# Two kinds of transpose leave TensorE: values and keys turned in 32x32 squares by VectorE and placed by GpSimd, with another window of dense steps before the corner products

## The chip, the cores and the metric

The kernel runs on one core of one Trainium2 chip. The number that counts is the device time of one execution in microseconds (us), as the median of several runs. A change of this size is read against the spread of these runs.

## The reference, cut to what matters

One layer of a two-branch backbone runs over 384 tokens (128 of context, 256 latent). One wide input projection feeds a bidirectional RWKV-7 scan (branch A) and a gated short convolution (branch B). Each branch is projected to the model width, the two are merged by gates and projected once more.

```python
z = h @ w_in                                   # 384 x 2048 by 2048 x about 22900, the bulk of the work
def step(S, inp):                              # branch A, per head, per direction, per token
    r_t, w_t, k_t, v_t, a_t, b_t = inp
    sa = einsum('dbhij,dbhj->dbhi', S, a_t)
    S = S * w_t[..., None, :] + sa[..., :, None] * b_t[..., None, :] + v_t[..., :, None] * k_t[..., None, :]
    y = einsum('dbhij,dbhj->dbhi', S, r_t)
y_a = (groupnorm(y) * lnx_g + lnx_b + bonus) * silu(g_a) @ w_out_a
y_b = (b_gate * conv3(c_gate * x_b) * silu(g_b)) @ w_out_b
out = x + gate * ((sigmoid(m_a) * y_a + sigmoid(m_b) * y_b) @ w_o)
```

The scan has 32 heads of 64 channels and two directions; its final context states are outputs too.

## The kernel before, in words

**Dense steps.** All large products run in one stream of dense steps. One step is three 128x128 by 128x384 matmuls (L81, L82, L83: high part by high part, high by low, low by high; the split into parts is made by ScalarE at L88 and VectorE at L89 for weights, elsewhere for data). A pair of weight column blocks is 32 steps. The stream holds pairs called rk (r and k of a block), gv (gate and v), bc, bx, bg, gb (branch B), ma, mb (merge gates), and at the end ob (output projection of B). What consumes a finished pair (L467 to L485 and others, VectorE and ScalarE) is issued beside it.

**Blocks.** The scan runs in 16 blocks of two heads. The sequence is cut into 6 chunks of 64 tokens, in each of 2 directions. Within a chunk the recurrence is a triangular system. For one block the work in program order is:

- `prep_b`: products pA of keys and queries (L703, TensorE), masked into the tile A by VectorE (L709, four for each direction). The two 32x32 diagonal triangles of each chunk go through DRAM into a tile U with the triangles on 48 partitions (`ui`, L713; `U`, L719). VectorE inverts them in 30 rounds of a product (L724) and a sum (L726): this is called the solve below. The result goes back through DRAM into A (`uo`), and VectorE turns one half of it into the tile x11 (L737, two instructions). Meanwhile GpSimd scales the keys `bk` in place (L716).
- `prep_c`: TensorE transposes the values v and the reversed values vr (L763, 2 x 3 of 128x128) and the scaled keys bk (L772, 10 of 128x128) by multiplying with the identity; ScalarE copies the results from PSUM into the lower half of `sav` (L765) and into `bt` (L773). Each group is followed by one dense step.
- `prep_a` of the next block: its keys, decays and queries.
- `scan`: products pav of A with the values (L850), the corner of the inverse (pH, L842, reads x11; later pX), a bonus product, and then two interleaved chains over the chunks (po L804, pq L821, pu L828) that carry the state; between these stand a few dense steps each.
- `norm` and, in the next block, `finish`: group norm, transposition back (py, L936), the gate (L939, L940), and a store to DRAM.

**Order.** TensorE's instructions keep the order in which the program issues them. `ds_.go(n)` issues n dense steps at that place. The constant `WINDOW` sets how many stand between the second pA and the corner of a block (`FIRST` and `LAST` add to it in the first and the last block). On the other engines a scheduler orders instructions by their readiness in its own model and by priority; an engine then runs them in that fixed order.

**The gate's wait.** Before `prep_a(b + 1)` the program issues dense steps until the pair gv of block b is done. In all, between the second pA and pav there are 87 dense steps in blocks 2 to 14 (six behind pA, `PB1`, and 81 more), 101 in block 1, 110 in block 0 and 102 in block 15.

**The tail.** After block 15's `finish` the rows of branch A come back from DRAM, one load (L507, tile `yst_a`, three buffers), one cast and one split (L509, tile `yal`) for each of 16 rows, and feed the output projection oa (tile d_oa). What is left of the pairs ob runs ahead of it.

Of the kernel before, what the change touches and what calls it, by code (L numbers as in the profile page):

```python
# [15 lines left out]
P = 128  # L16
D = 2048
KC = 16
T = 384
# [37 lines left out]
def hybrid_step(ctx, tc, cst, x_prompt, x_sample, state_f, state_b, c, c_ctx, ada_w, ada_b, norm_g,  # L57
# [35 lines left out]
    PB0, PB1, H0, H1, CH0, CH1 = 14, 6, 3, 4, 2, 4  # L93
    PRO, WINDOW, FIRST, LAST = 32, 80, 24, 16

# [313 lines left out]
    def tmp(nm):  # L409
        return box["sp"].tile([P, T], F32, tag="t", name=nm, bufs=8)  # L410
# [231 lines left out]
    def prep_k(b, o):  # L642
# [6 lines left out]
        for d in range(2):  # L649
# [15 lines left out]
            o["bn"].append(aa)  # L665

    def prep_b(b, o):

# [28 lines left out]
        for d in range(2):  # L697
# [7 lines left out]
            for n0, w in ((0, 4), (4, 2)):  # L705
                mk = cs[:, m0:m0 + P].rearrange("p (w t) -> p w t", t=C).unsqueeze(1).broadcast_to([P, w, 2, C])
                for h in range(2):
                    f0 = NCH * d + n0
                    V.tensor_tensor(A[:, :, f0:f0 + w, hss[h]].rearrange("p w n t -> p n w t"),  # L709
                                    pas[h, n0][:, 0:w, :].rearrange("p n (w t) -> p n w t", t=C), mk, ALU.mult)  # L710
            yield PB1
# [3 lines left out]
        for d in range(2):  # L715
            G.tensor_tensor(o["bk"][d][:], o["bk"][d][:], o["ep"][d][:, :, C:C + 1].broadcast_to([P, NCH, P]), ALU.mult)  # L716

# [21 lines left out]
    def prep_c(b, o):  # L739

        r, v, A = r_[b], v_[b], o["A"]

        s_in = sp.tile([P, 2, C], F32, tag="s_in", name=f"s_in_{b}")
        for d in range(2):
            for h in range(2):
                for jb in range(2):
# [3 lines left out]
                                      [:, :, 32 * jb:32 * jb + 32])  # L750

        sav = sp.tile([P, 2 * NCH, P], F32, tag="sav", name=f"sav_{b}")
        bt = sp.tile([P, 2 * NCH, P], F32, tag="bt", name=f"bt_{b}")
        o["sav"], o["bkt"] = sav, bt
        for d in range(2):
            if d == 0:
                src = v
            else:
                src = tmp(f"vr_{b}")
                S.copy(src[:], v[:, ::-1])  # L760
            pv = bank(f"pv_{b}_{d}")
            for q in range(3):
                TE.transpose(pv[:, q, :], src[:, q * P:(q + 1) * P], ident)  # L763
            for e in range(2):
                S.copy(sav[C:P, NCH * d + e:NCH * d + NCH:2, :], pv[C * e:C * e + C, 0:3, :])  # L765
            yield 1
        for d in range(2):

            for n0, n1 in (((0, 4), (4, 5)), ((0, 3), (4, 6)))[d]:
                pb = bank(f"pb_{b}_{d}_{n0}")  # L770
                for n in range(n0, n1):
                    TE.transpose(pb[:, n - n0, :], o["bk"][d][:, n, :], ident)  # L772
                S.copy(bt[:, NCH * d + n0:NCH * d + n1, :], pb[:, 0:n1 - n0, :])  # L773
                yield 1
        ks = o["kd"]
# [166 lines left out]

    def drive(gen, prio=0, at=None, fn=None):
        n = i = 0
        while True:
            if i == at:
                fn()
            i += 1
            with tc.high_priority(offset=prio):
                u = next(gen, None)  # L950
            if u is None:
                return n
            ds_.go(u)
            n += u
# [3 lines left out]
    drive(prep_a(0, cur))  # L958
    prep_k(0, cur)
    prev = None  # L960
    for b in range(NB):
# [10 lines left out]
        n = drive(prep_c(b, cur))  # L972
        nxt = {}
        if b < NB - 1:
            while f"gv{b}" not in ds_.done:
                ds_.go(1)
                n += 1
            n += drive(prep_a(b + 1, nxt))
        w = WINDOW + (FIRST if b == 0 else LAST if b == NB - 1 else 0)
        if n < w:  # L980
# [6 lines left out]

        drive(scan(b, cur), 300, 3 if b < NB - 1 else None, keys)
        norm(b, cur)
# [182 lines left out]
```

## Time and profile before

| what | value |
| --- | --- |
| median of 3 runs | 2237.07 us (2235.28 to 2239.02) |
| the profiled execution's own time | 2234.36 us |
| its span in the profile | 2232.6 us |
| TensorE busy | 2173.1 us, 97% |
| VectorE busy | 1553.3 us, 70% |
| ScalarE busy | 1013.5 us, 45% |
| GpSimd busy | 115.7 us, 5% |
| granted TensorE clock | 0.998 |

PE is TensorE, DVE VectorE, ACT ScalarE, POOL GpSimd, SP the engine that issues most transfers. A row of the timeline gives the start in us from the span's start, the busy time, the engine, the line of the kernel, the operation, the tiles (written <- read), the shapes, the count of instructions in a row, and in brackets how long the engine stood idle before it and what ended that. A row of the groups gives, after the count, the busy time and the mean of one instruction in ns, and then the idle time of the engine just before these instructions with its main releaser. Matmuls overlap: a dense matmul is shown with 0.33 us, while the next one starts 0.174 us later.

### The profile page before, as it was taken

Reading aid. Unit: us, or ns where it says so; the run is one execution under the profiler, and the core shown is the slowest. Engines: PE = TensorE matmul, PEld = TensorE weight load, DVE = VectorE, ACT = ScalarE, POOL = GpSimd, SP = SyncE. Lnnn points to the kernel's source line nnn. Section 1 sums busy time; section 2 is a strip of 40 time slices with the busy share of each in tenths; the row PEclk is TensorE's granted clock in tenths of the full one; section 3 lists DMA queues with packets and bytes.
Section 4 is the critical chain, followed back from the end, with each engine's and each line's share of the span. In section 5 each row is a group of like instructions: output and inputs, shape, how many; then the busy total and the mean of one; then the engine's idle time right before and its main releaser. Section 6 shows DMA issues by size and latency. Waiting matters only on the chain.

```text
span 2232.6 us, 40518 instructions
## 1 busy us (share of the span) xinstructions
PE 2173.1 (97%) x16020; PEld 2062.7 (92%) x16020; DVE 1553.3 (70%) x3240; ACT 1013.5 (45%) x1784; POOL 115.7 (5%) x113
## 2 busy tenths in 40 slices
PE   5999999999999999999999999999999999999998
PEld 3589999999999999999999999999999999998988
DVE  3259567787878878777878787887777785444354
ACT  4245435454545454444445454546454633333333
POOL 2000000000000000000000000000000000000000
PEclk9999999999999999999999999999999999999999
DMA  9974454444343435343444434344445464886633
GB/s 338 346 211 128 131 141 116 116 117 118 108 132 107 130 100 131 106 130 100 121 108 127 112 107 133 107 122 126 124 118 139 144 196 143 294 281 233 220 132 113
DMA packets 426574, 335.25 MB, mean 150 GB/s; under 512 B 82496, under 2 KB 408720, under 8 KB 425488
## 3 DMA queue, kind: packets, MB, share of 16 engines
q1 hardware_dynamic: 424896, 330.91, 50.2%
q8 instruction: 126, 2.06, 0.4%
q10 hardware_dynamic: 432, 1.57, 0.2%
q14 instruction: 64, 0.52, 0.1%
q0 software_dynamic: 1056, 0.19, 0.1%
HBM read 305.80 MB, written 26.21 MB: 149 GB/s over the span
## 4 chain that ended last, share of the span: by engine, by line
PE 74%; DVE 12%; DMA 6%; ACT 4%; issue 2%; SPq 1%; POOL 0%; POOLq 0%; DVEq 0%; ACTq 0%
DMA raw_adah<-in_ada_w_dram 4%; PE d_rk L81 3%; PE d_rk L82 3%; PE d_rk L83 3%; PE d_gv L81 3%; PE d_gv L82 3%; PE d_gv L83 3%; PE d_oa L81 2%; PE pA L703 2%; PE d_oa L83 2%; PE d_oa L82 2%; PE d_mb L81 2%; PE d_mb L83 2%; PE d_mb L82 2%; PE d_bc L81 2%
## 5 line engine op out<-in xcount | busy, mean ns | idle before, releaser
L724 DVE TENSOR_TENSOR ut<-U 48x30 f32<-48x30 f32 (+14 forms) x480 | 154.8, 323 | 18.3 <-DMA U<-ui 5.5
L81 PE MATMUL d_rk<-h_hi,whi_rk 128*128 128x384 f32 x480 | 161.7, 337 | 0.6 <-ACT lst L554 0.6
L726 DVE TENSOR_TENSOR U<-U,ut 48x30 f32<-48x30 f32 (+14 forms) x480 | 154.5, 322 | 11.1
L81 PE MATMUL d_gv<-h_hi,whi_gv 128*128 128x384 f32 x480 | 160.6, 335 | 0.0
L82 PE MATMUL d_rk<-h_lo,whi_rk 128*128 128x384 f32 x480 | 160.5, 334 | 0.0
L83 PE MATMUL d_rk<-h_hi,wlo_rk 128*128 128x384 f32 x480 | 160.4, 334 | 0.0
L83 PE MATMUL d_gv<-h_hi,wlo_gv 128*128 128x384 f32 x480 | 160.4, 334 | 0.0
L82 PE MATMUL d_gv<-h_lo,whi_gv 128*128 128x384 f32 x480 | 160.4, 334 | 0.0
L88 ACT CAST whi_gv<-raw_gv 128x1024 fp32r<-128x1024 f32 (+1 forms) x64 | 64.0, 999 | 139.6 <-PE d_rk L82 100.0
L88 ACT CAST whi_rk<-raw_rk 128x1024 fp32r<-128x1024 f32 x60 | 63.0, 1054 | 110.8 <-PE d_rk L82 34.7
L89 DVE TENSOR_TENSOR wlo_rk<-raw_rk,whi_rk 128x1024 fp32r<-128x1024 f32 x60 | 72.9, 1218 | 45.3 <-ACT whi_rk L88 35.6
L81 PE MATMUL d_bc<-h_hi,whi_bc 128*128 128x384 f32 x256 | 92.2, 360 | 0.0
L81 PE MATMUL d_gb<-h_hi,whi_gb 128*128 128x384 f32 x256 | 92.2, 360 | 0.0
L81 PE MATMUL d_bg<-h_hi,whi_bg 128*128 128x384 f32 x256 | 92.2, 360 | 0.0
L81 PE MATMUL d_bx<-h_hi,whi_bx 128*128 128x384 f32 x256 | 92.1, 360 | 0.0
L81 PE MATMUL d_ma<-h_hi,whi_ma 128*128 128x384 f32 x256 | 91.6, 358 | 0.0
L81 PEld LDWEIGHTS d_rk<-h_hi,whi_rk 128*128 128x128 f32 x480 | 90.1, 188 | 0.9 <-ACT lst L554 0.9
L81 PE MATMUL d_mb<-h_hi,whi_mb 128*128 128x384 f32 x256 | 90.4, 353 | 0.0
L81 PEld LDWEIGHTS d_gv<-h_hi,whi_gv 128*128 128x128 f32 x480 | 90.1, 188 | 0.2
L81 PE MATMUL d_ob<-ybh,whi_ob 128*128 128x384 f32 x256 | 88.4, 345 | 2.0 <-DVE smb L521 1.0
L82 PEld LDWEIGHTS d_rk<-h_lo,whi_rk 128*128 128x128 f32 x480 | 90.2, 188 | 0.0
L82 PEld LDWEIGHTS d_gv<-h_lo,whi_gv 128*128 128x128 f32 x480 | 90.1, 188 | 0.0
(315 smaller groups left out, 6548.4 us busy)
## 6 DMA issues: line engine op xcount, KB each, us to landing
raw_adah<-in_ada_w_dram SPq DMA_DIRECT2D x64, 512.0 KB, 8.7
raw_rk<-in_w_in_dram SPq DMA_DIRECT2D x60, 512.0 KB, 5.3
raw_gv<-in_w_in_dram SPq DMA_DIRECT2D x60, 512.0 KB, 4.9
raw_ma<-in_w_in_dram SPq DMA_DIRECT2D x16, 1024.0 KB, 5.6
raw_mb<-in_w_in_dram SPq DMA_DIRECT2D x16, 1024.0 KB, 5.6
raw_bc<-in_w_in_dram SPq DMA_DIRECT2D x16, 1024.0 KB, 5.5
raw_bx<-in_w_in_dram SPq DMA_DIRECT2D x16, 1024.0 KB, 5.4
raw_bg<-in_w_in_dram SPq DMA_DIRECT2D x16, 1024.0 KB, 5.5
```

The source lines that it names most:

```text
L81: TE.matmul(out, wh, xh, start=start, stop=False)
L82: TE.matmul(out, wh, xl, start=False, stop=False)
L83: TE.matmul(out, wl, xh, start=False, stop=stop)
L88: S.copy(hi[0:rows], src)
L89: V.tensor_tensor(lo[0:rows], src, hi[0:rows].bitcast(F32), ALU.subtract)
L703: TE.matmul(pas[h, n // 4 * 4][:, n % 4, :], bk[hss[h], n, :], pr[hss[h], n, :], start=True, stop=True)
L724: V.tensor_tensor(tv, U[:, 0:s, s:s + 1].broadcast_to([48, s, w]), U[:, s:s + 1, s + 1:].broadcast_to([48, s, w]), ALU.mult)
L726: V.tensor_tensor(U[:, 0:s, s + 1:], U[:, 0:s, s + 1:], tv, ALU.add)
```

## The change

Four things change.

1. **Values.** A new function `prep_v` lets VectorE turn v (and v read backwards) in 32x32 squares into two tiles `vt` (STREAM_TRANSPOSE, 128x384 each). For block b + 1 it is issued during the scan of block b, once the gate's pair of block b, which also carries the v of block b + 1, is done and four steps of the scan have been issued. GpSimd then places the squares with 16 copies per block into the lower half of `sav`.
2. **Keys.** After the last mask VectorE turns `bk` in place in 32x32 squares (two instructions of 128x768), behind GpSimd's scaling of it. GpSimd places the squares with 32 copies per block into `bt`. TensorE's 16 transposes per block (L763, L772) and ScalarE's 8 copies from PSUM (L765, L773) are gone, and with them the PSUM banks pv and pb.
3. **Window.** `prep_a(b + 1)` is issued once 12 steps (`PA`) are left in the window and the pair rk of block b + 1 is done; nothing waits for the gate's pair there. `WINDOW` goes from 80 to 86, `FIRST` from 24 to 18, `LAST` from 16 to 10. Between the second pA and pav there are now 92 dense steps in blocks 1 to 14, 110 in block 0 and 102 in block 15.
4. **Tail.** With more dense steps used up inside the blocks, fewer are left at the end: between the py of block 15's `finish` and the first matmul of oa there stood 84 dense steps of ob, and there are now 28. The first load of ob's rows moves from the start of block 15 into the scan of block 14. In SP's queue four loads of 1 MB for the adaptive gate (raw_adag) now stand between the loads of yst_a; the last of them, which waits for TensorE's products on its buffer, stands ahead of the last three loads of yst_a.

Over the whole program TensorE's rows fall from 11,362 to 11,266, VectorE's rise from 2935 to 3017, ScalarE's fall from 1501 to 1378, GpSimd's rise from 106 to 170.

```diff
-    PRO, WINDOW, FIRST, LAST = 32, 80, 24, 16
+    PRO, WINDOW, FIRST, LAST, PA = 32, 86, 18, 10, 12
...
+    def prep_v(b, o):
+
+        o["vt"] = []
+        for d in range(2):
+            x = sp.tile([P, T], F32, tag=f"vt{d}", name=f"vt_{b}_{d}")
+            V.transpose(x[:], v_[b][:, ::-1] if d else v_[b][:])
+            o["vt"].append(x)
...
-                    V.tensor_tensor(A[:, :, f0:f0 + w, hss[h]].rearrange("p w n t -> p n w t"),
-                                    pas[h, n0][:, 0:w, :].rearrange("p n (w t) -> p n w t", t=C), mk, ALU.mult)
+                    last = V.tensor_tensor(A[:, :, f0:f0 + w, hss[h]].rearrange("p w n t -> p n w t"),
+                                           pas[h, n0][:, 0:w, :].rearrange("p n (w t) -> p n w t", t=C), mk,
+                                           ALU.mult).ins
...
         for d in range(2):
-            G.tensor_tensor(o["bk"][d][:], o["bk"][d][:], o["ep"][d][:, :, C:C + 1].broadcast_to([P, NCH, P]), ALU.mult)
+            lam = G.tensor_tensor(o["bk"][d][:], o["bk"][d][:],
+                                  o["ep"][d][:, :, C:C + 1].broadcast_to([P, NCH, P]), ALU.mult).ins
+
+        with tc.issue_after(last):
+            for d in range(2):
+                V.transpose(flat(o["bk"][d][:]), flat(o["bk"][d][:]))
+        bt = sp.tile([P, 2 * NCH, P], F32, tag="bt", name=f"bt_{b}")
+        with tc.issue_after(lam):
+            for d, p, q in ((d, p, q) for d in range(2) for p in range(4) for q in range(4)):
+                put = G.tensor_copy(bt[32 * p:32 * p + 32, NCH * d:NCH * d + NCH, 32 * q:32 * q + 32],
+                                    o["bk"][d][32 * q:32 * q + 32, :, 32 * p:32 * p + 32]).ins
+
+        sav = sp.tile([P, 2 * NCH, P], F32, tag="sav", name=f"sav_{b}")
+        with tc.issue_after(put):
+            for d in range(2):
+                x = o["vt"][d][:].rearrange("p (n e t) -> p n e t", e=2, t=32)
+                for e in range(2):
+                    for q in range(4):
+                        G.tensor_copy(sav[C + 32 * e:C + 32 * e + 32, NCH * d:NCH * d + NCH, 32 * q:32 * q + 32],
+                                      x[32 * q:32 * q + 32, :, e, :])
+        o["sav"], o["bkt"] = sav, bt
...
-            pv = bank(f"pv_{b}_{d}")
-            for q in range(3):
-                TE.transpose(pv[:, q, :], src[:, q * P:(q + 1) * P], ident)
-            for e in range(2):
-                S.copy(sav[C:P, NCH * d + e:NCH * d + NCH:2, :], pv[C * e:C * e + C, 0:3, :])
-            yield 1
...
-                pb = bank(f"pb_{b}_{d}_{n0}")
-                for n in range(n0, n1):
-                    TE.transpose(pb[:, n - n0, :], o["bk"][d][:, n, :], ident)
-                S.copy(bt[:, NCH * d + n0:NCH * d + n1, :], pb[:, 0:n1 - n0, :])
-                yield 1
...
+        w = WINDOW + (FIRST if b == 0 else LAST if b == NB - 1 else 0)
         if b < NB - 1:
-            while f"gv{b}" not in ds_.done:
+            while n < w - PA or f"rk{b + 1}" not in ds_.done:
                 ds_.go(1)
                 n += 1
             n += drive(prep_a(b + 1, nxt))
...
+        def values():
+            with tc.issue_after(cur["turn"][1]):
+                prep_v(b + 1, nxt)
+
-        drive(scan(b, cur), 300, 3 if b < NB - 1 else None, keys)
+        drive(scan(b, cur), 300, ((3, f"rk{b + 1}", keys), (3, f"gv{b}", values)) if b < NB - 1 else ())
```

Three places show how the instructions move. The first is TensorE's order in block 5, behind the second group of pA. Before, the transposes of the values stand between dense steps of the pair bg, and those of the keys follow:

```order
L763 MATMUL pv_0_7535<-cs,v_6704 128x128 x3
L81 MATMUL d_bg_0_7252<-h_hi_79,whi_bg_1_1_7260 128x384
L82 MATMUL d_bg_0_7252<-h_lo_83,whi_bg_1_1_7260 128x384
L83 MATMUL d_bg_0_7252<-h_hi_79,wlo_bg_1_1_7261 128x384
L763 MATMUL pv_1_7547<-cs,vr_7545 128x128 x3
L81 MATMUL d_bg_1_7253<-h_hi_79,whi_bg_1_1_7260 128x384
L82 MATMUL d_bg_1_7253<-h_lo_83,whi_bg_1_1_7260 128x384
L83 MATMUL d_bg_1_7253<-h_hi_79,wlo_bg_1_1_7261 128x384
L772 MATMUL pb_0_0_7556<-cs,bk_0_7294 128x128 x4
```

The same place of the change, from the last pA on:

```order
L711 MATMUL pA_1_0_4_7544<-pr_1_7431,bk_1_7432 128x128
L711 MATMUL pA_1_1_4_7545<-pr_1_7431,bk_1_7432 128x128
L81 MATMUL d_bg_0_7336<-h_hi_79,whi_bg_1_1_7344 128x384
L82 MATMUL d_bg_0_7336<-h_lo_83,whi_bg_1_1_7344 128x384
L83 MATMUL d_bg_0_7336<-h_hi_79,wlo_bg_1_1_7345 128x384
L81 MATMUL d_bg_1_7337<-h_hi_79,whi_bg_1_1_7344 128x384
```

What moved: L763 and L772 (16 transposes per block) are gone, and dense steps follow one another.

The second place is VectorE's order in block 7, from the last mask to the first rounds of the solve. Before:

```order
L709 TENSOR_TENSOR A_9656<-pA_1_1_4_9711,cs 128x2x2x64
L89 TENSOR_TENSOR wlo_rk_0_1_9688<-raw_rk_0_9680,whi_rk_0_1_9687 128x1024
L89 TENSOR_TENSOR wlo_rk_1_0_9890<-raw_rk_1_9886,whi_rk_1_0_9889 128x1024
L724 TENSOR_TENSOR ut_9752<-U_9750 48x30
L726 TENSOR_TENSOR U_9750<-U_9750,ut_9752 48x30
```

The change (masks are at L717 and the solve at L753 and L755 there):

```order
L717 TENSOR_TENSOR A_9874<-pA_1_1_4_9932,cs 128x2x2x64
L730 STREAM_TRANSPOSE bk_0_9808<-bk_0_9808 128x768
L730 STREAM_TRANSPOSE bk_1_9814<-bk_1_9814 128x768
L89 TENSOR_TENSOR wlo_bx_1_1_9909<-raw_bx_1_9902,whi_bx_1_1_9908 128x1024
L89 TENSOR_TENSOR wlo_rk_0_0_10133<-raw_rk_0_10129,whi_rk_0_0_10132 128x1024
L753 TENSOR_TENSOR ut_10025<-U_10023 48x30
L755 TENSOR_TENSOR U_10023<-U_10023,ut_10025 48x30
```

What moved: the two transposes of the keys stand between the last mask and the solve, and a split of bx that stood elsewhere comes behind them.

The third place is VectorE's order some rounds into the solve of the same block. Before, one split stands between the rounds:

```order
L724 TENSOR_TENSOR ut_9752<-U_9750 48x150
L726 TENSOR_TENSOR U_9750<-U_9750,ut_9752 48x6x25
L724 TENSOR_TENSOR ut_9752<-U_9750 48x168
L89 TENSOR_TENSOR wlo_rk_1_1_9894<-raw_rk_1_9886,whi_rk_1_1_9893 128x1024
L726 TENSOR_TENSOR U_9750<-U_9750,ut_9752 48x7x24
L724 TENSOR_TENSOR ut_9752<-U_9750 48x184
L726 TENSOR_TENSOR U_9750<-U_9750,ut_9752 48x8x23
L724 TENSOR_TENSOR ut_9752<-U_9750 48x198
```

The change, at the same rounds:

```order
L755 TENSOR_TENSOR U_10023<-U_10023,ut_10025 48x4x27
L753 TENSOR_TENSOR ut_10025<-U_10023 48x130
L89 TENSOR_TENSOR wlo_rk_0_1_10137<-raw_rk_0_10129,whi_rk_0_1_10136 128x1024
L467 TENSOR_TENSOR bc_0_9852<-bc_0_9852,d_bx_0_9900 128x384
L755 TENSOR_TENSOR U_10023<-U_10023,ut_10025 48x5x26
L753 TENSOR_TENSOR ut_10025<-U_10023 48x150
L755 TENSOR_TENSOR U_10023<-U_10023,ut_10025 48x6x25
L473 SCALAR_TENSOR_TENSOR bu_0_10177<-bc_0_9852,par,bu_0_10177 128x127
L473 SCALAR_TENSOR_TENSOR bu_0_10177<-bc_0_9852,par,bu_0_10177 128x4x63
L475 SCALAR_TENSOR_TENSOR bu_0_10177<-bc_0_9852,par,bu_0_10177 128x127
L475 SCALAR_TENSOR_TENSOR bu_0_10177<-bc_0_9852,par,bu_0_10177 128x4x63
L753 TENSOR_TENSOR ut_10025<-U_10023 48x168
```

What moved: a split, the product of bc with bx and the pieces of the convolution (bu) now stand between rounds of the solve.

More of the change, by code (lines that the diff above doesn't have):

```diff
@@ L739, in prep_c @@
     def prep_c(b, o):
-        r, v, A = r_[b], v_[b], o["A"]
+        r = r_[b]
         s_in = sp.tile([P, 2, C], F32, tag="s_in", name=f"s_in_{b}")
@@ L750, in prep_c @@
                                       [:, :, 32 * jb:32 * jb + 32])
[L752 to L760, printed above, removed]
-            pv = bank(f"pv_{b}_{d}")
-            for q in range(3):
-                TE.transpose(pv[:, q, :], src[:, q * P:(q + 1) * P], ident)
-            for e in range(2):
-                S.copy(sav[C:P, NCH * d + e:NCH * d + NCH:2, :], pv[C * e:C * e + C, 0:3, :])
-            yield 1
-        for d in range(2):
-            for n0, n1 in (((0, 4), (4, 5)), ((0, 3), (4, 6)))[d]:
-                pb = bank(f"pb_{b}_{d}_{n0}")
-                for n in range(n0, n1):
-                    TE.transpose(pb[:, n - n0, :], o["bk"][d][:, n, :], ident)
-                S.copy(bt[:, NCH * d + n0:NCH * d + n1, :], pb[:, 0:n1 - n0, :])
-                yield 1
         ks = o["kd"]
@@ L941, in finish, with drive @@
         nc.sync.dma_start(ya_d[b], ya[:])
-    def drive(gen, prio=0, at=None, fn=None):
+    def drive(gen, prio=0, late=()):
         n = i = 0
+        late = list(late)
         while True:
-            if i == at:
-                fn()
+            for x in [x for x in late if i >= x[0] and x[1] in ds_.done]:
+                x[2]()
+                late.remove(x)
             i += 1
@@ L951, in drive @@
             if u is None:
+                assert not late
                 return n
@@ L959, in hybrid_step @@
     prep_k(0, cur)
+    prep_v(0, cur)
     prev = None
@@ L978, in hybrid_step @@
             n += drive(prep_a(b + 1, nxt))
-        w = WINDOW + (FIRST if b == 0 else LAST if b == NB - 1 else 0)
         if n < w:
```

## The prediction

> **What bounds the kernel now.** I read the page's totals first, then its slices, its chain of waits, and last the groups and the timeline of single blocks.
>
> ```profile
> span 2232.6 us, 40518 instructions
> PE 2173.1 (97%) x16020; PEld 2062.7 (92%) x16020; DVE 1553.3 (70%) x3240; ACT 1013.5 (45%) x1784; POOL 115.7 (5%) x113
> PE   5999999999999999999999999999999999999998
> PE 74%; DVE 12%; DMA 6%; ACT 4%; issue 2%; SPq 1%; POOL 0%; POOLq 0%; DVEq 0%; ACTq 0%
> ```
>
> TensorE (PE) is full from the second slice on and carries three quarters of the chain that ended last. So an instruction taken from PE is time saved, as long as PE does not then stand waiting. The 12% of DVE in that chain say where such a wait would come from. Once in each block DVE must finish a long serial solve before PE's corner products may start:
>
> ```profile
> 735.68 1.95 DVE L709 TENSOR_TENSOR A<-pA,cs 128x512 f32<-128x512 f32 x4 [0.65 <-PE pA L703]
> 736.28 1.49 POOL L716 TENSOR_TENSOR bk<-bk,ep 128x768 f32<-128x768 f32 x1 [3.37 <-PE pA L703]
> 746.08 0.18 DVE L724 TENSOR_TENSOR ut<-U 48x30 f32<-48x30 f32 x1 [0.30 <-DMA U<-ui]
> 775.12 0.20 DVE L726 TENSOR_TENSOR U<-U,ut 48x30 f32<-48x30 f32 x1
> 782.78 1.14 DVE L737 STREAM_TRANSPOSE x<-A 32x384 f32<-32x384 f32 x2 [1.40 <-DMA A<-uo]
> 787.37 0.62 PE L842 MATMUL pH<-x,A 32*32 32x32 f32 x48
> ```
>
> This is block 5: masks until 737.6, the triangles through DRAM, 29.2 us of solve, back through DRAM, and x11 ready at 783.9. PE comes to pH at 787.4, so 3.5 us of the cover of dense steps are unused. I call that the block's margin. Other blocks have as much, or none:
>
> ```profile
> 681.65 1.02 DVE L737 STREAM_TRANSPOSE x<-A 32x384 f32<-32x384 f32 x2 [2.15 <-DMA A<-uo]
> 682.37 0.76 PE L842 MATMUL pH<-x,A 32*32 32x32 f32 x48
> ...
> 992.87 1.17 DVE L737 STREAM_TRANSPOSE x<-A 32x384 f32<-32x384 f32 x2 [1.16 <-DMA A<-uo]
> 997.70 0.62 PE L842 MATMUL pH<-x,A 32*32 32x32 f32 x48
> ...
> 1726.86 1.03 DVE L737 STREAM_TRANSPOSE x<-A 32x384 f32<-32x384 f32 x2 [1.20 <-DMA A<-uo]
> 1731.65 0.62 PE L842 MATMUL pH<-x,A 32*32 32x32 f32 x48
> ```
>
> Block 4 has -0.3 us (682.37 against 681.65 + 1.02; the first products of pH need only the first of the two x11 instructions, so it lost next to nothing), block 7 has 3.7, block 14 has 3.8. Read in the same way, blocks 2 to 15 have 0.9, 2.3, -0.3, 3.5, 1.0, 3.7, 0.0, 1.2, 1.8, 2.7, 0.8, 2.2, 3.8 and 0.4. Blocks 0 and 1 have 17.5 and 9.0.
>
> **What leaves PE.** A dense matmul starts every 0.174 us. Between 739.08 and 739.76 stand two such starts and three transposes of L763:
>
> ```profile
> 739.08 0.34 PE L83 MATMUL d_bg<-h_hi,wlo_bg 128*128 128x384 f32 x1
> 739.26 0.49 PE L763 MATMUL pv<-cs,v 128*128 128x128 f32 x3
> 739.76 0.34 PE L82 MATMUL d_bg<-h_lo,whi_bg 128*128 128x384 f32 x1
> L772 PE MATMUL pb<-cs,bk 128*128 128x128 f32 x160 | 27.9, 272 | 0.2 <-issue 0.2
> L763 PE MATMUL pv<-cs,vr 128*128 128x128 f32 x48 | 7.9, 272 | 1.4 <-DVE A L709 1.4
> L763 PE MATMUL pv<-cs,v 128*128 128x128 f32 x48 | 7.8, 271 | 0.0
> ```
>
> So three transposes cost 0.68 - 0.35 = 0.33 us, 0.11 each; the 272 ns of the groups overlap their neighbours. The groups count 160 + 48 + 48 = 256: 256 x 0.11 = **-28.2 us**. L763 also waited 1.4 us in all: **-1.4**. ScalarE loses 128 copies; nothing waits for it there, so this counts as nothing.
>
> **The window.** It grows from 87 to 92 steps of 3 x 0.174 = 0.52 us in blocks 2 to 14 and loses 16 x 0.11 = 1.76 us of transposes. PE thus arrives at the corner only 2.6 - 1.76 = 0.85 us later after pA. The steps themselves are not new work; they come from the tail. With 0.5 us for the half of x11 that may be late, a block's usable margin is its margin + 1.35. Block 1 loses 9 steps and 1.8 us, 6.5 us in all, of its 9.0. Block 15 keeps 102 steps and loses 1.76: 0.4 + 0.5 - 1.8 = -0.9.
>
> **New work on DVE.** The trace has no transposes of 128x768; the nearest rows give a slope.
>
> ```profile
> L737 DVE STREAM_TRANSPOSE x<-A 32x384 f32<-32x384 f32 x32 | 17.4, 558 | 25.3 <-DMA A<-uo 25.1
> L782 DVE STREAM_TRANSPOSE st<-s_in 64x64 f32<-64x64 f32 x64 | 12.2, 221 | 0.6
> ```
>
> 0.56 us for 384 and 0.22 for 64 make about 0.97 for 768 if the slope holds; twice the 0.56 is the upper end, 1.1. Two of them behind the masks end near 739.7 in block 5, over 6 us before U has come from DRAM (746.08): hidden by that round trip. Of the two transposes of v per block, 0.56 each, 30 stand in the scan, where PE's po waits for DVE already:
>
> ```profile
> L804 PE MATMUL po<-st,pr 128*128 128x128 f32 x320 | 49.5, 277 | 7.6 <-DVE st L833 7.6
> ```
>
> At worst each delays a chain, 30 x 0.56 = 17; at best nothing. Nine waits in 320 make 7.6 us, so most chains have slack: **+1.5**, from 0 to 17.
>
> **What moves into the solve.** DVE runs its queue in order, so whatever stands between the rounds of the solve delays x11 by its own time. The order of the change shows more there in some blocks, as in block 7, shown above. Prices:
>
> ```profile
> L89 DVE TENSOR_TENSOR wlo_rk<-raw_rk,whi_rk 128x1024 fp32r<-128x1024 f32 x60 | 72.9, 1218 | 45.3 <-ACT whi_rk L88 35.6
> 719.20 0.74 DVE L473 SCALAR_TENSOR_TENSOR bu<-bc,par,bu 128x127 f32<-128x127 f32 x2
> 720.50 0.55 DVE L467 TENSOR_TENSOR bc<-bc,d_bx 128x384 f32<-128x384 f32 x1
> L724 DVE TENSOR_TENSOR ut<-U 48x30 f32<-48x30 f32 (+14 forms) x480 | 154.8, 323 | 18.3 <-DMA U<-ui 5.5
> L726 DVE TENSOR_TENSOR U<-U,ut 48x30 f32<-48x30 f32 (+14 forms) x480 | 154.5, 322 | 11.1
> ```
>
> A split is 1.22, a piece of bu 0.37, a full 128x384 tile 0.55. More than before stand, net of what leaves: in block 7 two splits, eight pieces, three tiles: 2.4 + 3.0 + 1.6 = 7.0; in block 2 one split, four pieces, three tiles: 4.4; in block 9 two splits and six tiles: 5.7; in block 13 one split, two tiles, four pieces: 3.8; in block 15 two tiles: 1.1. Block 5 has 2.9 more, within its margin; the others at most 2.2. DVE's own pauses between the rounds can take little of that: 18.3 + 11.1 - 5.5 = 23.9 us in 16 blocks, 1.5 a block, and I count none of it.
>
> **GpSimd's copies.** No copy of 32 partitions by 192 elements is in the trace, nor a DVE transpose beside it. Bounds for one copy:
>
> ```profile
> 146.51 0.56 POOL L579 MEMSET st<- 128x256 f32 x2 [38.77 <-PE pe L83]
> 147.01 1.52 POOL L584 MEMSET ep<- 128x390 f32 x4
> ```
>
> 0.38 us for 390 elements and 0.28 for 256 make 0.75 ns an element on a base of 0.09: 0.23 for 192. L716's product takes 1.49 for 768, 1.94 ns an element: 0.46. A copy reads one tile, a memset none and the product two, so I take 0.30. 48 copies from about 739.7 on then end near 754, at 0.46 near 762: long before pav near 787, so they are not late. But they run beside the solve, and this pair shows that DVE and GpSimd can block each other:
>
> ```profile
> 304.59 1.49 POOL L716 TENSOR_TENSOR bk<-bk,ep 128x768 f32<-128x768 f32 x1 [5.21 <-PE pA L703]
> 305.22 1.27 DVE L940 TENSOR_TENSOR ya<-ya,ga 128x384 f32<-128x384 f32 x1
> 731.00 0.56 DVE L940 TENSOR_TENSOR ya<-ya,ga 128x384 f32<-128x384 f32 x1
> ```
>
> L940 alone takes 0.56 (731.00). At 305.22 it took 1.27, and ended 0.41 behind L716's end at 306.08: it began in effect 0.15 before L716 was through. L940 has two inputs in SBUF, as have the solve's products and sums. By 746.1 some 21 copies are done and 27 left, so up to 31 with a late start. Each may hold a DVE instruction by nothing, if the two slip past each other, or by 0.30 - 0.15 = 0.15: 0 to 4.6 us a block, call it c. Only a copy that starts first can block, and the pauses of 1.5 us a block take some of it. I take **c = 1.0**, 0.03 a copy, nearer the lower end for these two reasons. The Trainium skill, page "SBUF — State Buffer", section "SBUF: two separate sides", says that a DVE instruction with two inputs in SBUF and a GpSimd instruction that reads SBUF lock each other out for the whole instruction, without sharing. By that rule in full the 31 copies would hold the solve 31 x 0.30 = 9.3 us a block. The trace agrees that the later one is blocked, and shows about 0.15 us of overlap.
>
> **The corner's sum.** Overrun = new work + c - usable margin: block 2: 4.4 + 1.0 - 2.3 = 3.1; block 7: 7.0 + 1.0 - 5.0 = 3.0; block 9: 5.7 + 1.0 - 2.6 = 4.1; block 13: 3.8 + 1.0 - 3.6 = 1.2; block 15: 1.1 + 1.0 + 0.9 = 3.0; the others none: **+14.4**. Bounds: 2 with c = 0 and the pauses of 1.5 us used up in each of the five blocks (14.4 - 5.0 - 7.5), 44 with c = 4.
>
> **The tail.**
>
> ```profile
> 1890.64 0.52 PE L936 MATMUL py<-cs,ytok 128*128 128x128 f32 x3 [0.21 <-DVE ytok L930]
> 1937.66 0.33 PE L81 MATMUL d_oa<-yah,whi_oa 128*128 128x384 f32 x1
> L507 SPq DMA_DIRECT2D yst_a<-ya_d x16: 319/320/844, 1897.5 to 1925.0; - x16
> L509 DVE TENSOR_TENSOR yal<-yst_a,yah x16: 549/558/560, 1900.4 to 1929.3; 128x384 fp32r<-128x384 f32 x16
> 1890.00:1938.00 48.00, 45.66 (x260) 44.41 (x259) 26.33 (x39) 19.00 (x29) 1.08 (x2) 1.00 0.85 281
> ```
>
> Behind py, PE has 47.0 us of dense steps before d_oa. 56 fewer take 29.1 away: oa's first step comes at +17.9. It needs row 0 then, which was there at 1900.4 + 0.6, +10.4. Row 15 is needed some 27 steps later, at +31.9, and was ready at 1929.3 + 0.6, +39.2: 7.3 late. The loads come one by one, 0.85 of the DMA engines are busy there (281 GB/s), and the last three now stand behind a gate load: **+8**. Bounds: 3, since fewer weights are loaded beside them, and 14, if the gate load's wait costs another 6 as its 13 steps of oa do.
>
> **Sum** on the profiled execution's 2234.4: -28.2 - 1.4 + 1.5 + 14.4 + 8 = -5.7, so 2228.7. The median of the runs is 2.7 above it: **2231**.
>
> **Rivals.** *Full gain.* The pauses between the rounds swallow 1.5 us of what moved in, and copies slip past. Corner 2, tail 5, chain 0: 2234.4 - 29.6 + 7 + 2.7 = **2214**. For it: the margins of blocks 5, 7 and 14. Against: 1.5 us in 60 rounds are 0.025 each, too short for a piece of 0.37 or more to fit in.
>
> *GpSimd takes back the gain.* The copies hold the solve by c = 4. Every block from 2 on but 10 and 14 then overruns, in the same sum: 6.1 + 1.6 + 1.7 + 2.1 + 2.8 + 6.0 + 1.7 + 7.1 + 2.2 + 2.1 + 4.2 + 6.0 = 44: 2234.4 - 29.6 + 1.5 + 44 + 8 + 2.7 = **2261**. It turns slower than 2241.5 at corner 25, from c = 2.5 on (0.08 us a copy). For it: L940's 0.7 us of blocking. Against: one such pair only.
>
> *The lock in full.* With c = 9.3, 5.3 us more in twelve blocks, and 10 in blocks 10 and 14 together: 44 + 64 + 10 = 118: **2335**. That is what the rule of the Trainium skill's page named above gives. Against: L940's overlap, and that most copies would have to start just ahead of an instruction of the solve.
>
> *The gain cancels out.* With c = 2 the same sum gives a corner of 21 and 2234.4 - 29.6 + 1.5 + 21 + 8 + 2.7 = **2238**: PE's freed time turns into waits, and the change doesn't do what it says.
>
> **How the numbers follow.** Likeliest, 2222 to 2237: 0.42. Full gain, 2208 to 2222: 0.27. Cancels out, 2237 to 2241.5: 0.08. GpSimd, 2241.5 to 2270: 0.18. Lock in full: 0.05. A measurement of this kernel tells 0.2%, 4.5 us, from no change. Faster (under 2232.6) is the full gain and 0.26 of the likeliest: 0.53. Same is the likeliest's other 0.16 and 0.08: 0.24. Slower: 0.23. The range of 8 in 10 is 2210 to 2262.
>
> **What would show it.** Right: L763 and L772 gone from PE with some 28 us fewer of transposes; x11's L737 ends behind PE's arrival at pH in blocks 2, 7, 9, 13 and 15 by 1 to 4 us, and PE's idle before L842 names it; d_oa's steps wait for yal by 8 us in all. The solve's single rounds beside GpSimd keep their length but for a few tenths a block. Wrong: rounds of the solve twice as long while copies run (c), idle time before L842 in nearly all blocks, a wait of sav or bt for GpSimd, or po's wait for st grown well over 7.6.

## The result, and the profile after

The changed kernel takes 2272.86 us (median of 4 runs, 2269.61 to 2273.21) against 2237.74 us before (4 runs, 2235.28 to 2239.02): ratio 1.0155, 95% interval 1.0137 to 1.0173. It is 35 us slower, where 6 us faster was forecast. The profiled execution took 2273.21 us.

The page's totals of the changed kernel:

```profile
span 2271.4 us, 40600 instructions
PE 2168.4 (95%) x15764; PEld 2052.9 (90%) x15764; DVE 1638.1 (72%) x3304; ACT 938.8 (41%) x1627; POOL 561.3 (25%) x881
```

PE's instructions fell by 256, the transposes (six merged rows a block, so the 96 rows named ahead). Yet its busy time fell by 4.7 us only, not by 28. Span less busy time, PE's idle time, rose from 59.5 to 103.0 us. So two things ate the gain: 43.5 us more of waiting, and matmuls that took longer; the mean granted clock fell from 0.998 to 0.987. If the 28.2 us of transposes left as worked out, PE's remaining work took about 23.5 us longer. The clock can be taken from the trace directly. It is 1.00 or 0.50 there, and half of PE's busy time at 0.50 is 21.7 us, against 1.7 us before. So 20.0 us of the 23.5 are the clock; the cause of the other 3.5 stays open.

What PE waited for, from the list of waits (us in total, times, the longest; the prologue's waits left out):

```profile
PE pl L83 <- DVE lwl L89: 8.4, 5, 2.9
PE d_ob L81 <- ACT ybh L508: 6.8, 1, 6.8
...
PE d_bg L81 <- DVE ga L440: 6.0, 2, 4.8
PE po L809 <- DVE st L838: 6.0, 8, 1.7
PE d_gb L81 <- DVE ga L440: 4.5, 2, 2.4
PE d_oa L81 <- ACT yah L508: 4.5, 3, 3.8
PE d_oa L82 <- DVE yal L509: 3.5, 4, 0.9
PE d_bc L81 <- DVE bg L486: 3.4, 1, 3.4
PE d_ob L82 <- DVE ybl L509: 3.2, 2, 2.6
...
PE pH L847 <- DVE x L766: 0.3, 1, 0.3
```

Three groups are new. Dense steps wait for ga, bg and bc, which are VectorE's work on finished pairs. The products pl of the next block's keys wait for the split lwl (1.7 us before, 8.4 now). ob waits for its first rows, oa for its own. The corner itself, pH, waits 0.3 us in all.

Where the dense steps' wait comes from, on the timeline in block 6, PE and VectorE (rows of one engine each, in order of time):

```profile
891.79 0.34 PE L83 MATMUL d_bg<-h_hi,wlo_bg 128*128 128x384 f32 x1
896.89 0.69 PE L81 MATMUL d_bg<-h_hi,whi_bg 128*128 128x384 f32 x1 [4.77 <-DVE ga L440]
897.38 0.52 PE L82 MATMUL d_bg<-h_lo,whi_bg 128*128 128x384 f32 x1
897.70 0.52 PE L83 MATMUL d_bg<-h_hi,wlo_bg 128*128 128x384 f32 x1
...
893.23 1.21 DVE L89 TENSOR_TENSOR wlo_bg<-raw_bg,whi_bg 128x1024 fp32r<-128x1024 f32 x1
894.36 0.38 DVE L755 TENSOR_TENSOR U<-U,ut 48x228 f32<-48x228 f32 x1
...
896.30 0.54 DVE L440 TENSOR_TENSOR ga<-ga,d_gv 128x384 f32<-128x384 f32 x1
```

The pair gv was finished before bg began. Its gate half lies in one of the three PSUM banks of the dense stream until VectorE's L440 has read it. L440 stands in VectorE's queue among the late rounds of the solve and runs at 896.30. PE, which needs the bank for the second half of bg, stands 4.77 us. Behind that wait the matmuls start every 0.32 us instead of 0.174. The next view shows it as the clock (a stretch of 10 us, PE busy, and third from the end the granted clock); the last two stretches are those around ob's start:

```profile
890.00:900.00 10.00, 5.23 (x22) 4.80 (x21) 9.62 (x24) 2.83 (x5) 2.79 (x7) 0.80 0.36 106
900.00:910.00 10.00, 10.00 (x51) 10.00 (x50) 7.04 (x20) 3.47 (x5) 0.00 (x0) 0.85 0.41 126
1790.00:1800.00 10.00, 2.63 (x16) 2.03 (x14) 9.94 (x17) 6.58 (x14) 0.00 (x0) 0.86 0.46 144
1800.00:1810.00 10.00, 7.31 (x23) 6.69 (x24) 8.81 (x19) 4.91 (x12) 0.00 (x0) 0.50 0.63 203
```

What makes VectorE's solve longer, from the groups of GpSimd's copies and of the solve:

```profile
L734 POOL COPY bt<-bk 32x192 f32<-32x192 f32 x512 | 262.1, 512 | 42.2 <-DVE bk L730 21.5
L743 POOL COPY sav<-vt 32x192 f32<-32x192 f32 x256 | 178.8, 699 | 11.5
L753 DVE TENSOR_TENSOR ut<-U 48x30 f32<-48x30 f32 (+14 forms) x480 | 175.3, 365 | 29.2 <-DMA U<-ui 17.9
L755 DVE TENSOR_TENSOR U<-U,ut 48x30 f32<-48x30 f32 (+14 forms) x480 | 174.0, 362 | 11.6
```

The head of the solve in block 5, on the timeline:

```profile
748.56 16.70 POOL L734 COPY bt<-bk 32x192 f32<-32x192 f32 x32 [1.28 <-DVE bk L730]
754.81 0.33 DVE L753 TENSOR_TENSOR ut<-U 48x30 f32<-48x30 f32 x1
755.17 0.35 DVE L755 TENSOR_TENSOR U<-U,ut 48x30 f32<-48x30 f32 x1
```

The solve's instructions take 365 and 362 ns where they took 323 and 322. That is 960 x 0.041 = 39 us in 16 blocks, 2.5 us a block. The first ones, beside the copies, take 0.33 and 0.35 where block 5 had 0.18 for each before.

### The profile page after: what moved, and what is told of

Same layout as the page of the kernel before. It is cut to its first block, busy times and chain, and to the rows that moved or that the text cites. A ratio compares the mean times of both kernels' runs of the same rounds, so it can differ in the third digit from the quotient of the medians.

```text
span 2271.4 us, 40600 instructions
## 1 busy us (share of the span) xinstructions
PE 2168.4 (95%) x15764; PEld 2052.9 (90%) x15764; DVE 1638.1 (72%) x3304; ACT 938.8 (41%) x1627; POOL 561.3 (25%) x881
## 3 DMA queue, kind: packets, MB, share of 16 engines
q8 instruction: 124, 2.03, 0.4%
## 5 line engine op out<-in xcount | busy, mean ns | idle before, releaser
L734 POOL COPY bt<-bk 32x192 f32<-32x192 f32 x512 | 262.1, 512 | 42.2 <-DVE bk L730 21.5
L753 DVE TENSOR_TENSOR ut<-U 48x30 f32<-48x30 f32 (+14 forms) x480 | 175.3, 365 | 29.2 <-DMA U<-ui 17.9
L934 POOL TENSOR_TENSOR rs<-var,nhalf 128x6 f32<-128x6 f32 x16 | 22.5, 1405 | 696.1 <-DVE var L932 696.1
L755 DVE TENSOR_TENSOR U<-U,ut 48x30 f32<-48x30 f32 (+14 forms) x480 | 174.0, 362 | 11.6
L743 POOL COPY sav<-vt 32x192 f32<-32x192 f32 x256 | 178.8, 699 | 11.5
L868 POOL MEMSET A<- 64x1536 f32 x16 | 22.0, 1376 | 356.1 <-issue 326.2
L81 PE MATMUL d_oa<-yah,whi_oa 128*128 128x384 f32 x256 | 87.5, 342 | 4.5 <-ACT yah L508 4.5
```

The costliest lines, as they stand in the source:

```text
L81: TE.matmul(out, wh, xh, start=start, stop=False)
L734: put = G.tensor_copy(bt[32 * p:32 * p + 32, NCH * d:NCH * d + NCH, 32 * q:32 * q + 32], o["bk"][d][32 * q:32 * q + 32, :, 32 * p:32 * p + ...
L743: G.tensor_copy(sav[C + 32 * e:C + 32 * e + 32, NCH * d:NCH * d + NCH, 32 * q:32 * q + 32], x[32 * q:32 * q + 32, :, e, :])
L753: V.tensor_tensor(tv, U[:, 0:s, s:s + 1].broadcast_to([48, s, w]), U[:, s:s + 1, s + 1:].broadcast_to([48, s, w]), ALU.mult)
L755: V.tensor_tensor(U[:, 0:s, s + 1:], U[:, 0:s, s + 1:], tv, ALU.add)
L868: G.memset(A[C:P, 0, :, :], 0.0)
```

## The experiments

All times are medians, with the kernel before run beside them on the same chip; its own medians there lie between 2237.18 and 2238.91 us, so a difference of two changed kernels from different chips can be off by 2 us. Theory A, which the expectations name: one half of the loss comes from VectorE being late (by GpSimd's copies and by work moved into the solve), the other from where ob and oa now begin. The rivals are lettered as they come.

**The window alone.** Edit, on the kernel before:

```diff
-    PRO, WINDOW, FIRST, LAST = 32, 80, 24, 16
+    PRO, WINDOW, FIRST, LAST, PA = 32, 86, 18, 10, 12
-            while f"gv{b}" not in ds_.done:
+            while n < w - PA or f"rk{b + 1}" not in ds_.done:
```

> The kernel before with only the window's part of the change: 86 steps, first 18, last 10, no wait for the gate's pair. Values and keys stay on TensorE, GpSimd places nothing. Theory A (the loss has two halves: VectorE late by GpSimd's copies and by work moved into the solve, and a start of ob and oa that lost its cover by the window): ob's first steps wait about 10 us for their rows, oa's about 7, the clock dips behind both, and no dense step waits for ga, bg or bc: about 2258, from 2250 to 2266. Rival B (all of the loss comes from GpSimd's copies): 2235 to 2242.

Measured: 2264.06 us against 2237.18, ratio 1.0119 (1.0104 to 1.0134). So 27 of the 35 us come without any offload. Its totals, its waits, and the stretch of 10 us behind ob's start:

```profile
PE 2187.9 (97%) x16020; PEld 2070.0 (91%) x16020; DVE 1557.3 (69%) x3240; ACT 1000.0 (44%) x1771; POOL 117.5 (5%) x113
```

```profile
PE d_ob L81 <- ACT ybh L508: 6.9, 1, 6.9
PE d_oa L81 <- ACT yah L508: 3.9, 3, 3.1
PE d_oa L82 <- DVE yal L509: 3.3, 4, 0.9
PE d_ob L82 <- DVE ybl L509: 2.9, 2, 2.0
```

```profile
1790.00:1800.00 10.00, 7.89 (x26) 7.09 (x27) 8.76 (x20) 5.30 (x14) 0.00 (x0) 0.51 0.69 215
```

PE does the same work as before and is busy 14.8 us longer: ob's 9.8 us and oa's 7.2 us of waiting come with a slow clock behind them, here 0.51. By the sum used above, 12.3 of the 14.8 us are the clock. Rival B, that all comes from GpSimd, falls. Two small waits came that theory A had not: 1.2 us for bg and 0.2 for ga.

**The offload without the copies.** GpSimd's two loops of copies are replaced by two memsets; bt and the lower half of sav hold zeros, so what the scan computes is left out.

> The changed kernel with GpSimd's 48 copies per block left out; two memsets write zeros to bt and to the lower half of sav, so scan and output are not those of the reference. VectorE's transposes and its order stay. Theory A: the solve's own instructions fall from 0.36 to 0.32 us, the solve by 2 to 3 us a block; dense steps' waits on ga, bg and bc fall from 18 us to under 8; ob and oa wait as in the change: 2245 to 2258. Rival C (what moved into the solve and the late loads are all of it, the copies cost nothing): 2266 to 2274.

Measured: 2242.75 us against 2237.18, ratio 1.0029 (1.0018 to 1.0041), a little under theory A's range. Four of its seven runs lie at 2241.7 to 2242.8 us and three at 2246.6 to 2247.5, so it is 25 to 31 us under the changed kernel; the profile, of a run of 2247.02 us, is 26 us under that of the change. The solve:

```profile
L746 DVE TENSOR_TENSOR ut<-U 48x30 f32<-48x30 f32 (+14 forms) x480 | 154.4, 322 | 27.9 <-DMA U<-ui 17.0
L748 DVE TENSOR_TENSOR U<-U,ut 48x30 f32<-48x30 f32 (+14 forms) x480 | 154.4, 322 | 11.3
```

322 ns, as before. Waits for ga fall from 13.1 us to 1.9; those for bg (3.4) and bc (2.0) stay, as do those of ob (9.9) and oa (8.1). Of the 26 us between the two profiles 18 are waits of PE and 8 its longer busy time. The solves are 39 us longer in all with the copies, so about half of that lateness reaches PE as waiting. Rival C falls. A later run, with the same copies elsewhere, tells how much of this comes from their place.

**The copies on ScalarE.** In both loops `G.tensor_copy` becomes `S.copy`.

> The changed kernel with the 48 copies per block on ScalarE in place of GpSimd. If blocking between GpSimd and VectorE is what makes the solve late, the solve's instructions are back at 0.32 us and the time is that of the kernel without copies or a little above, 2245 to 2262. If it is the copies as such, wherever they run (they come late, or ScalarE's casts of weights come late behind them), it stays at 2268 or more.

Measured: 2353.64 us, ratio 1.0515 (1.0499 to 1.0531). The time is that of the second branch, but for a reason that says nothing against blocking: the solve's instructions are back at 322 ns, as the first branch has it. PE now waits 13.0 us for whi_gv, 9.2 for whi_rk, 18.8 for r: ScalarE's casts of the weights stand behind the copies. That ScalarE was at 41% on average didn't help.

**The old sizes of the window, with the offload.** 80, 24, 16 in place of 86, 18, 10.

> The changed kernel with the old sizes of the window (80, first 24, last 16; still no wait for the gate's pair). Theory A: ob begins at about its old place and waits under 3 us for its rows (10 before), oa under 2 (8 before), their dips of the clock go; the corner has 3.1 us less cover in blocks 1 to 14 and loses 10 to 25 us at pH: 2250 to 2268. Rival: the corner's cover is worth more than the tail's, 2275 or more.

Measured: 2289.41 us, ratio 1.0232 (1.0216 to 1.0247). Theory A's number fails, the rival's holds. ob's wait for rows and oa's wait are gone as expected, but the corner waits 17.2 us at pH, dense steps wait 20.5 us for ga (13.1 in the change), and the clock is slow for more of the span (0.983). With longer windows the late VectorE shows at the banks; with shorter ones it shows there and at the corner too. Theory A counted the waits at pH and left out that those for ga would grow and the clock with them.

**Own buffers for the rows of ob and oa.** Two edits, tried on the window's part alone and on the changed kernel:

```diff
-        yload(yb_d, box["ybh"], box["ybl"], "b", tmp)
+        yload(yb_d, ..., "b", lambda nm: box["sp"].tile([P, T], F32, tag="yst_b", name=nm, bufs=2))
-    ... tag="yst", name=nm, bufs=3))
+    ... tag="yst", name=nm, bufs=6))
```

> The window's part alone (values and keys on TensorE), with two buffers of their own for the rows that ob loads (before, they take turns in a ring of eight tiles that the next block's keys use too) and six buffers in place of three for the rows that oa loads. Theory A: ob's wait of 9.8 us and its slow clock go nearly whole, oa's wait of 7.2 us at least by half: 2237 to 2250. Rival D (the loads wait for the transfers themselves, not for a buffer): 2260 or more.

> The changed kernel with the same two edits on the loads of ob and oa, all else as in the change. Theory A: what the edits give to the window alone they give here too, since the blocks before are not touched: 2273 less 14 to 26, 2247 to 2259. Rival: the late VectorE holds the rows of ob all the same (less than 6 us gained).

Measured: 2266.22 us (ratio 1.0129, 1.0114 to 1.0144) and 2271.83 us (1.0160, 1.0143 to 1.0176): nothing gained, as the numbers of both rivals had it. The waits changed their names. Those of the window's part alone:

```profile
PE d_ob L82 <- DVE ybl L509: 5.6, 3, 4.4
PE pg L292 <- DMA raw_adag<-in_ada_w_dram: 5.4, 1, 5.4
PE d_ob L81 <- ACT ybh L508: 5.3, 4, 2.7
```

ob's first row now comes in time and waits 4.4 us for VectorE's split, which stands behind the keys of block 15; some of the next rows still come late. In all ob waits 10.9 us, where it waited 9.8. oa's rows come in time and the gate's weights come late instead. More buffers alone do not take the waits away, and rival D's reason, the transfers themselves, isn't what ob's longest wait shows.

**Values placed early; and values alone.** On the kernel with the two edits above, the values' copies move to the start of `prep_b`. In the second one the keys are back on TensorE.

> As the kernel with the two edits on the loads, and the 16 copies of the values are issued at the start of a block, ahead of the products pA, no longer behind the 32 copies of the keys. Theory A (only copies that run beside the solve cost): a third of the copies leaves the solve, the solve's instructions lose a third to a half of their 0.04 us, dense steps wait less for ga: 5 to 15 us under that kernel, 2236 to 2250. Rival E (the copies cost through something else, such as their own lateness): no change within 4 us.

> As the kernel with the early values, but the keys stay on TensorE (10 transposes and 4 copies by ScalarE per block, as before); values by VectorE and GpSimd. Theory A: no copy runs beside the solve, so its instructions take 0.32 us as before; TensorE saves 96 transposes, 10.6 us, and loses what the window's part with mended loads loses: 2228 to 2242, under the kernel with the keys off TensorE. Rival: keys on GpSimd are worth their 17.6 us on TensorE, and this kernel is slower than that one.

Measured: 2290.92 us (1.0244, 1.0222 to 1.0267) and 2290.01 us (1.0249, 1.0227 to 1.0272). The times don't answer what these two kernels were made for, for a reason of their own. In GpSimd's order the early copies stand ahead of L933, the power of the group norm. So VectorE's normalisation waits, and PE's py behind it. The waits and the groups of the kernel with early values:

```profile
PE py L940 <- DVE ytok L934: 21.4, 15, 2.8
```

```profile
L934 DVE TENSOR_TENSOR ytok<-ytok,rs 128x384 f32<-128x384 f32 x16 | 8.9, 558 | 60.9 <-POOL rs L933 60.9
```

What the values alone are worth off TensorE stays open. The solve itself is as theory A had it. With a third of the copies gone from beside it, its instructions take 350 and 348 ns (365 and 362 with all); with none beside it, 321.

**Cover given up in block 0 alone.** On the kernel before, only `FIRST` goes from 24 to 86.

> The kernel before with one number changed: 86 in place of 24 extra steps in the window of block 0, where 17 us of cover are unused. It brings ob forward into block 14 (64 steps, against 56 in the change) and leaves 20 steps of ob in the tail (28 in the change, 84 before); every later block keeps its window, or loses a wait for the gate's pair. Theory A (the window's part costs by where ob and oa begin): waits for ybh and ybl, for yah and yal, and slow clock behind them as in the change: 2258 to 2275. Rival F (it is the windows of 92 steps or the later keys of the next block): 2236 to 2245.

Measured: 2246.42 us against 2238.59, ratio 1.0035 (1.0022 to 1.0048). It lost 8 us, between theory A's 20 and rival F's nothing. oa waits 8.3 us as expected; ob's rows wait 2.1 us, not 10. So being early is not what costs ob 10 us; two later runs are about that place. What this run lost goes with a thin tail, 20 steps of ob, and agrees with the 8 us that the prediction put on it.

**The copies moved out of the solve.** The values' copies stand behind the norm of the block before; those of the keys behind a small GpSimd copy that reads U after the solve:

```diff
+        with tc.issue_after(box["rs"]) if "rs" in box else ExitStack():   # after yield PB0: 16 copies to sav
...
         V.tensor_scalar(dg, dg, 1.0, None, ALU.add)
+        gdi = G.tensor_copy(gd[:], U[:, 0, 0:1]).ins
+        with tc.issue_after(gdi):                                         # 32 copies to bt
```

> The changed kernel with GpSimd's copies moved out of the solve: those of the values behind the group norm of the block before, ahead of pA; those of the keys behind the end of the solve (an instruction of GpSimd that reads U stands ahead of them). Windows as in the change. Theory A: the solve's instructions are back at 0.32 us, waits of dense steps for ga nearly gone, ob and oa wait as in the change: 2240 to 2252, as without the copies. Rival E (the copies cost by being late, or wherever they run): 2262 or more.

Measured: 2251.93 us against 2238.59, ratio 1.0055 (1.0040 to 1.0070): 21 us under the changed kernel, with the same copies.

```profile
L749 DVE TENSOR_TENSOR ut<-U 48x30 f32<-48x30 f32 (+14 forms) x480 | 157.5, 328 | 32.3 <-DMA U<-ui 21.4
L751 DVE TENSOR_TENSOR U<-U,ut 48x30 f32<-48x30 f32 (+14 forms) x480 | 158.1, 329 | 11.3
```

328 and 329 ns: rival E falls. About 21 of the copies' 25 to 31 us come from running beside the solve; the few that are left between this kernel and the one without copies stay open.

**Other sizes, with the copies beside the solve and without.** `WINDOW, FIRST, LAST` = 84, -10, 15 brings ob back to block 15 and leaves 83 steps of ob in the tail; block 0 pays with cover it didn't use.

> The changed kernel with other sizes of the window: 84, first -10, last 15, so that ob begins at block 15 again and 83 steps of ob stand in the tail. Copies run beside the solve as in the change. Theory A: ob's and oa's waits and their slow clock are gone (25 us); the corner has 1 us less cover in blocks 2 to 14 and loses 5 to 10: 2250 to 2262. Rival: as with the old window, 2280 or more.

> Both edits: copies outside the solve, and the window of 84, first -10, last 15. Theory A: TensorE keeps most of its 28 us; what moved into the solve still costs 5 to 10: 2212 to 2230, faster than the kernel before. Rival (the offload is worth nothing even without blocking): 2236 or more.

Measured: 2251.22 us (1.0056, 1.0041 to 1.0071) and 2229.39 us (0.9962, 0.9948 to 0.9976). Both lie in theory A's ranges, the second near its upper end. The two halves add up: 21.6 us for the sizes, 20.9 for the copies' place, 43.5 for both.

**Which step ob begins at.** What the window's part alone costs was still open after the run with 86 in block 0. Two runs on the window's part alone: `FIRST` 26 in place of 18, and the sizes 84, -10, 15.

> The window's part alone with 26 in place of 18 extra steps in block 0: ob begins 8 steps earlier in block 14's scan, ahead of the bonus product and of VectorE's work on the keys of block 15, and 20 steps of ob stand in the tail (28 before). Theory G (the place decides: there the rows of ob are loaded and cast ahead of that work): ob's waits fall from 9.8 to about 2 us, slow clock by 5 or more, oa waits 3 to 4 us more: 2246 to 2256. Rival (windows of 92 steps): 2262 or more.

> The window's part alone with the sizes 84, -10, 15: ob begins at block 15 as in the kernel before, 83 steps of ob in the tail; windows of 90 steps in blocks 1 to 14 and no wait for the gate's pair. Values and keys on TensorE. Theory G: within 4 us of the kernel before, 2234 to 2243. Rival (longer windows cost by themselves): 2250 or more.

Measured: 2254.22 us (1.0066, 1.0051 to 1.0081) and 2243.28 us against 2238.91 (1.0018, 1.0009 to 1.0027). Eight steps earlier, ob waits 4.1 us instead of 9.8, and the kernel is 10 us faster although oa waits a little longer (7.8 us). With ob back at block 15, 4 of the 27 us are left, just over theory G's range; that remainder is at the edge of what these runs can tell. So of the 27 us, some 23 come from where ob begins and how thin the tail is, and not from windows of 90 steps. By the run with 86 in block 0, about 8 of them are the thin tail.

**One step further.** The faster kernel with `LAST` 21.

> The kernel with the copies moved out of the solve and the window of 84, -10, 15, with 21 in place of 15 extra steps in block 15, six more ahead of its corner and six fewer in the tail. Theory A: block 15's wait at pH of 3.1 us and its slow clock of 3 us go: 2223 to 2229. Rival: the tail loses as much, 2229 to 2234.

Measured: 2226.22 us against 2238.91, ratio 0.9943 (0.9926 to 0.9960): the best of the study, 12.7 us under the kernel before. Its gain over the step before, some 3 us, is not clear of the spread, but the wait at pH did go (3.6 us to 0.5). The largest waits left behind the prologue are po's for the chain's st (4.6 in ten pieces), those of dense steps for ga (4.5) and bu (2.7), and that of pl for lwl (3.0).

## Why the prediction was wrong

**What it had right.** 256 transposes left PE, and they were worth what was forecast: with the slow clock taken off as above, PE is busy 2146.7 us, and 2173.8 with the window's part alone, 27 us more (28.2 forecast). The transposes of the keys on VectorE take 0.96 us (0.97 was worked out), and start behind the last mask. The chain suffered little: po waits for st 6.0 us where it waited 7.6, and pq for sav 2.9 where it waited 0.8 (2.4 with the window's part alone). oa's wait was forecast at 8 us and is 4.5 + 3.5 = 8.0, though more than half of it is for yah, ScalarE's cast, where all was forecast for yal. Whether what moves into the solve was sized right can't be told: in the kernel without copies, waits of 3.4 us for bg and 2.0 for bc remain, but in the scans of blocks 10 and 3, where the prediction had no overrun.

**The step that failed first: "The steps themselves are not new work; they come from the tail."** This priced the tail, but not the other end of the same shift. ob's begin moves into block 14's scan, which the order showed, and it was costed at nothing. There ScalarE and VectorE are busy with the keys of block 15, and ob's first rows come 10.0 us late, with the clock at half speed for the ten us behind. The window's part alone costs 27 us, and 23 of them go when ob begins at block 15 again and the tail is as long as before.

**Blocking, c.** Taken at 1.0 us a block, it is 2.5, inside its bounds (0 to 4.6). The shortest copies take 0.33 us and the median 0.34 (0.30 was taken), and an early instruction of the solve is held 0.15 us, as was worked out from the one pair in the old trace (0.30 - 0.15). The value was put near the lower end because "Only a copy that starts first can block" and DVE's pauses take some of it. That was too little weight for what the trace shows: beside the copies every one of the solve's first instructions is longer. The Trainium skill, page "SBUF — State Buffer", section "SBUF: two separate sides", says that the loser of such a pair is blocked for the whole instruction of the other. The runs bear out who blocks whom: the solve is at 322 ns without copies and at 328 with the copies elsewhere. They do not bear out the size, since that rule gave 9.3 us a block.

**The place of the overrun.** The prediction let VectorE's lateness arrive at pH, in blocks 2, 7, 9, 13 and 15. The same formula with c = 2.5 gives a corner of 26 us instead of 14.4, and PE waits 0.3 us at pH. The waits that did come, for ga, bg, bc, lwl and at py, are 27 us more than before. That the two totals are near is luck. In blocks 7, 9, 13 and 15, where the formula has 17 of its 26 us, these waits come to 2.1 us. Of the 27 us, 10.4 are there without copies, and 4.5 with the window's part alone, where GpSimd places nothing and VectorE takes over no transposes. Not the end of the solve is what PE meets first, but the work queued inside it: block 6's L440 releases a PSUM bank, and PE stops 4.77 us for it before the corner. By the time PE comes to that block's pH, x11 is there (timeline of the changed kernel):

```profile
915.15 0.56 DVE L766 STREAM_TRANSPOSE x<-A 32x384 f32<-32x384 f32 x1
916.46 0.62 PE L847 MATMUL pH<-x,A 32*32 32x32 f32 x48
```

The term's lower bound of 2 us also lets block 13 count as less than nothing; without that it is 3.2.

**The term that was not there: a wait costs more than its length.** The sum counted idle time alone. About 20 us of the loss is PE busy at a lower clock, nearly all of it behind waits of 2 us and more. With c = 2.5 (11 us more), ob's start (10.0, where it was 1.4) and the clock (20.0), the sum of 2228.7 comes to 2268.5; the profiled execution took 2273.2, and the 4.7 us between are open. This account is made afterwards, and its corner term fits in total only. What the runs show apart is 21 us for the place of the copies and some 22 for the sizes of the window; the clock's part shows only in the profiles.

The rival "GpSimd takes back the gain" came nearest: slower, at 2261, by the mechanism that no copies, or copies elsewhere, undo. It had c too high (4) and knew nothing of ob or the clock.

## What to carry to other kernels

Work that leaves the busiest engine isn't free on an idle one: GpSimd's copies cost through VectorE's long serial solve, and the kernel was 21 us faster as soon as they ran ahead of and behind it. When a constant gives more cover to one place, follow it to both ends of the stream it is taken from: which stage begins earlier, beside whose work, and what covers the stage behind. An instruction queued inside a late stretch is late too, and what waits for it, here the release of a PSUM bank, can stop the main engine before the stretch's own consumer does.

## What was not expected of the hardware

Short waits of PE lower its clock for a while. A wait of 4.77 us came with 0.80 and 0.85 in two stretches of ten us; the begin of ob, 6.8 and 2.6 us, with one at 0.50. It doesn't go by the length alone. The wait for ytok, up to 1288.10, is 1.98 us long and comes with 0.93 and 0.90. A wait of 2.03 us before 600.92 comes with 1.00 on both sides (the changed kernel, timeline and stretches):

```profile
1288.10 0.52 PE L941 MATMUL py<-cs,ytok 128*128 128x128 f32 x3 [1.98 <-DVE ytok L935]
600.92 0.44 PE L81 MATMUL d_bg<-h_hi,whi_bg 128*128 128x384 f32 x1 [2.03 <-DVE bc L467]
```

```profile
590.00:600.00 10.00, 8.89 (x60) 8.57 (x58) 9.83 (x20) 7.26 (x18) 0.00 (x0) 1.00 0.33 105
600.00:610.00 10.00, 9.08 (x60) 9.08 (x60) 9.71 (x26) 5.28 (x11) 0.00 (x0) 1.00 0.08 12
...
1280.00:1290.00 10.00, 8.02 (x53) 7.56 (x53) 6.26 (x14) 3.19 (x6) 1.32 (x1) 0.93 0.40 102
1290.00:1300.00 10.00, 10.00 (x76) 9.40 (x75) 7.73 (x14) 2.10 (x2) 3.77 (x5) 0.90 0.23 51
```

In the kernel without copies the same wait for bc, of the same 2.03 us, does come with a lower clock:

```profile
590.00:600.00 10.00, 7.97 (x43) 7.96 (x43) 8.63 (x23) 5.50 (x13) 0.00 (x0) 0.83 0.04 6
```

The trace's clock record shows a difference between them. The clock is at 0.50 in pieces of 3.41 us or a multiple, and the starts of these pieces lie a multiple of 3.41 us apart (466.02, 896.10 and 1288.63 us: 126 and 115 of them between). On that grid the wait for ytok and the one without copies lie whole in one piece, 58% and 59% of it, and the next piece is at 0.50. A border of the grid, at 599.13, cuts the wait before 600.92 into 0.24 and 1.79 us, and neither piece is followed by a slow one. So where a wait falls on the grid matters beside its length; the share of a piece that is enough stays open.

The Trainium skill, page "TensorE: Matmul & The Clock Gate", section "What's actually happening", gives a whole idle window of about 3.4 us as what lowers the clock; here a wait of 1.98 us was enough. VectorE and GpSimd slow each other on both sides. The row of the keys' copies by line (shortest, median and longest in ns) has a median of 0.34 us, where their mean is 0.51, and an instruction of the solve takes 0.04 us more in the mean. With the copies moved out of the solve the means fall, from 0.51 to 0.46 for the keys and from 0.70 to 0.52 for the values.

```profile
L734 POOL COPY bt<-bk x512: 332/342/5994, 197.5 to 1868.3; 32x192 f32<-32x192 f32 x171
```
